# Batched A·Bᵀ in fp32: one start-up wait moved from TensorE to VectorE, and the closing waits moved from GpSimd to SyncE

## The chip, the cores and the metric

The kernel runs on one core of one Trainium2 chip. The time is the device time of one execution in microseconds. For the kernel before, six runs gave a median of 127.28 us, from 126.77 to 127.58 us. One further execution was profiled; it took 126.67 us.

## The reference

Sixteen independent products of 512 x 512 matrices are computed. Inputs and outputs are float32; the kernel multiplies in bf16 and accumulates in fp32.

```python
def reference(a, b):            # a: 16 x 512 x 512, b: 16 x 512 x 512
    return np.matmul(a, b.transpose(0, 2, 1)).astype(np.float32)
```

Both factors have their contraction index last. [...] 33.55 MB are read from HBM and 16.78 MB are written.

## The kernel before

The batch is worked off in 8 pairs of matrices. For each pair, one 2 MB transfer brings in the two matrices of `a` and another one the two of `b`; a transfer fills one of seven `ld` buffers, with 8 consecutive rows of the pair on each of the 128 partitions. The first transfer of `a` and the first of `b` are split into two halves of 1 MB, with a semaphore for each half (`s_ld` and `s_second`).

The kernel is written out by hand: every engine has its own list of instructions, and semaphores are the only link between the lists. All of it stands in one critical section, and a second, very short section follows it.

- SyncE (SP) issues all loads and all stores but the first, in the order of the string `ORDER` (L32). Nine load instructions stand at its head and wait for nothing. Each later load waits until its buffer has been read (L89, L91), and each store waits until its output block has been evicted (L104). SP works in order, so a store that waits holds the loads behind it.
- VectorE (DVE) casts each load to bf16, in two halves (L116 and L121), into `ha` for `a` and `hb` for `b`. The first half of a cast raises `s_half`; the second raises `s_ca` or `s_cb`. It also evicts the transposes of `b` (L126).
- TensorE (PE) runs a hardware loop of 8 rounds (L172). In each it does 64 transposes of 128 x 128 (L185), through the identity matrix `ident`, and 32 matmuls of 128 x 512 (L199). Its first instruction in each round waits for `s_ca`. [...]
- ScalarE (ACT) evicts the transposes of `a` (L137) and the products (L153), and issues the store of product 0 (L163).
- GpSimd (POOL) builds the identity at the start: a memset (L67) and a select (L69), each of which raises `s_set` by one.

PE's list begins with a wait for `s_set` to be 2 (L171), ahead of the loop.

The end has two parts. When an engine has finished its list in the first section, it takes part in an exchange of semaphores that all five engines run between the sections (L40 in the profile). In the second section (L212 to L214), GpSimd waits for the last seven stores, 9 to 15, each in one of the seven buffers `ob` with its own semaphore `s_st`. After that the program has a closing barrier of all engines (L240), which also clears the semaphores.

Of the kernel before, what the change touches and what calls it, by code (L numbers as in the profile page):

```python
# [10 lines left out]
def kernel(  # L11
# [6 lines left out]
    nc = tc.nc  # L18
    P = 128
    batch, M, K = a.shape  # L20
# [8 lines left out]
    NO = 7  # L29
# [7 lines left out]
    def sem(name):  # L37
        return tc.alloc_semaphore(name)

    with tc.tile_critical(no_gpsimd_drain=True):  # L40
# [10 lines left out]
        s_set = sem("s_set")  # L51
        s_ld = [sem(f"s_ld{i}") for i in range(NL)]
        s_second = [sem(f"s_second{i}") for i in range(2)]
        s_st = [sem(f"s_st{i}") for i in range(NO)]
# [24 lines left out]
        for what in ORDER:  # L79
            if what == "L":  # L80
                u, slot = n_ld // 2, n_ld % NL
                src = (a if n_ld % 2 == 0 else b)[2 * u:2 * u + 2].rearrange(
                    "e (p j) k -> (e p) j k", j=2 * J
                )
                if n_ld >= NL:

                    v = (n_ld - NL) // 2
                    if (n_ld - NL) % 2 == 0:
                        nc.sync.wait_ge(s_half, 2 * v + 2)  # L89
                    else:  # L90
                        nc.sync.wait_ge(s_tb, KO * v + 1)  # L91
                if n_ld < 2:
                    nc.sync.dma_start(
                        ld[slot][:, :J, :], src[:, :J, :]
                    ).then_inc(s_ld[slot], 16)
                    nc.sync.dma_start(
                        ld[slot][:, J:, :], src[:, J:, :]
                    ).then_inc(s_second[slot], 16)
                else:
                    nc.sync.dma_start(ld[slot][:], src).then_inc(s_ld[slot], 16)  # L100
                n_ld += 1
            else:
                slot = n_st % NO
                nc.sync.wait_ge(s_out, n_st + 1)  # L104
                nc.sync.dma_start(
                    out[n_st].rearrange("(p j) n -> p j n", j=J), ob[slot][:]
                ).then_inc(s_st[slot], 16)
                n_st += 1

        for u in range(pairs):
            for x, (h, s_c) in enumerate(((ha, s_ca), (hb, s_cb))):
                n = 2 * u + x
                nc.vector.wait_ge(s_ld[n % NL], 16 * (n // NL + 1))
                nc.vector.tensor_copy(  # L116
                    out=h[:, :J, :], in_=ld[n % NL][:, :J, :]
                ).then_inc(s_half, 1)
                if n < 2:
                    nc.vector.wait_ge(s_second[n], 16)  # L120
                nc.vector.tensor_copy(  # L121
                    out=h[:, J:, :], in_=ld[n % NL][:, J:, :]
                ).then_inc(s_c, 1)
            for ko in range(KO):
                nc.vector.wait_ge(s_tb, KO * u + ko + 1)
                nc.vector.tensor_copy(  # L126
                    out=tb[:, ko, :],
                    in_=tp[:, (2 * ko + 1) % 4].rearrange("k j p -> k (j p)"),
                ).then_inc(s_eb, 1)
# [38 lines left out]
        def take(s, n):  # L168
            nc.tensor.wait_ge(s, n).then_inc(s, -n)  # L169

        nc.tensor.wait_ge(s_set, 2)  # L171
        with nc.Fori(  # L172
            0, pairs, engines=[nc.tensor.engine], head_slot={nc.tensor.engine: 24}
        ):
# [33 lines left out]
                    t.then_inc(s_mm, 1)  # L208

    with tc.tile_critical(no_gpsimd_drain=True):  # L212
        for n in range(batch - NO, batch):
            nc.gpsimd.wait_ge(s_st[n % NO], 16 * (n // NO + 1))  # L214


# [28 lines left out]
```

## Time and profile before

| what | before |
|---|---|
| median of 6 runs | 127.28 us |
| lowest and highest run | 126.77 and 127.58 us |
| the profiled execution, whole | 126.67 us |
| its span, first to last instruction | 124.9 us |
| granted TensorE clock, mean | 0.982 |
| PE, DVE, ACT, POOL busy | 72%, 47%, 57%, 1% |
| data moved | 50.37 MB, 403 GB/s over the span |

The page of a profile lists the busy time of each engine, and cuts the span into 40 slices in which one digit is the busy share in tenths; the row named DMA is the mean over the core's 16 DMA engines. Its last parts name groups of instructions by source line, and DMA issues with the time from issue to landing. Further views of the trace used here are: the waits (who waited for whom), the instructions of one source line, the timeline, the DMA queues in a window of time, and the busy times in chosen windows. All times in them count from the span's first instruction. A name such as SPq or POOLq is the engine's sequencer: the instructions that only wait, branch or issue. A transfer of this kernel is split over the 16 DMA engines, and each adds one to the transfer's semaphore when its share has landed, so that the sixteenth part sets the landing.

### The profile page before, as it was taken

What the parts mean: (1) busy time and instruction counts of PE and PEld (TensorE: products, weight loads), DVE (VectorE), ACT (ScalarE), POOL (GpSimd) and SP (SyncE); (2) the same over time, 40 slices, a digit from 0 to 9 for tenths busy, and PEclk for the clock granted to TensorE, in tenths of its full rate; (3) what the DMA queues carried; (4) which work ended last, traced back from release to release, by engine and by line L of the source; (5) the groups of instructions that cost most, each with busy time, mean ns of one, the idle gap of its engine ahead of it and who ended that gap; (6) DMA issues with size and microseconds to landing.
All of it is one profiled execution on the core that took longest, in us unless ns stands there. A gap on an engine that the chain in (4) does not pass through costs nothing. (4 is left out here: it accounts for less than half of the span.)

```text
span 124.9 us, 1959 instructions
## 1 busy us (share of the span) xinstructions
PE 89.9 (72%) x768; PEld 56.7 (45%) x768; DVE 59.2 (47%) x64; ACT 70.7 (57%) x129; POOL 0.7 (1%) x6
## 2 busy tenths in 40 slices
PE   0003089799789969996999699969776999698000
PEld 0002089347644754484449345934374458343000
DVE  0034534971794287648905980690566566300000
ACT  4001225468937885696669567947755769567000
POOL 2000000000000000000000000000000000000000
PEclk9999999999999999999999999999999999999975
DMA  3999999999999999999999999999999999999980
GB/s 92 394 422 441 436 436 436 420 430 373 401 422 417 462 396 430 417 430 441 415 441 430 388 443 420 401 443 415 454 428 425 415 428 425 425 422 428 425 349 16
DMA packets 4899, 50.37 MB, mean 403 GB/s; under 512 B 544, under 2 KB 544, under 8 KB 544
## 3 DMA queue, kind: packets, MB, share of 16 engines
q1 hardware_dynamic: 4752, 49.29, 94.2%
q10 hardware_dynamic: 144, 1.05, 2.0%
q8 instruction: 1, 0.02, 0.0%
q14 instruction: 2, 0.02, 0.0%
HBM read 33.55 MB, written 16.78 MB: 403 GB/s over the span
## 5 line engine op out<-in xcount | busy, mean ns | idle before, releaser
L199 PE MATMUL ps<-tb,ta 128*128 128x512 bf16 x256 | 56.5, 379 | 8.3 <-PEq L169 8.3
L153 ACT COPY ob<-ps 128x512 f32<-128x512 f32 x64 | 37.5, 586 | 26.4 <-PE ps L199 26.4
L137 ACT COPY ta<-tp 128x512 bf16<-128x512 bf16 x64 | 32.6, 625 | 17.7 <-PE tp L185 17.7
L199 PEld LDWEIGHTS ps<-tb,ta 128*128 128x128 bf16 x256 | 24.5, 98 | 37.8 <-issue 9.4
L126 DVE COPY tb<-tp 128x1024 bf16<-128x1024 bf16 x32 | 22.1, 691 | 28.7 <-PE tp L185 28.7
L185 PE MATMUL tp<-ident,ha 128*128 128x128 bf16 x256 | 21.2, 230 | 11.1 <-PEq L169 11.1
L185 PE MATMUL tp<-ident,hb 128*128 128x128 bf16 x256 | 21.0, 228 | 5.8 <-PEq L169 5.8
L185 PEld LDWEIGHTS tp<-ident,ha 128*128 128x128 bf16 x256 | 17.1, 104 | 13.7 <-issue 11.1
L185 PEld LDWEIGHTS tp<-ident,hb 128*128 128x128 bf16 x256 | 16.9, 103 | 6.3 <-issue 6.3
L116 DVE CAST hb<-ld 128x2048 bf16<-128x2048 f32 x8 | 9.8, 1223 | 9.3 <-DMA ld<-in_b_dram 9.3
L116 DVE CAST ha<-ld 128x2048 bf16<-128x2048 f32 x8 | 9.8, 1219 | 7.0 <-DMA ld<-in_a_dram 7.0
L121 DVE CAST ha<-ld 128x2048 bf16<-128x2048 f32 x8 | 9.8, 1220 | 2.2 <-DMA ld<-in_a_dram 2.2
L121 DVE CAST hb<-ld 128x2048 bf16<-128x2048 f32 x8 | 9.8, 1220 | 1.3 <-DMA ld<-in_b_dram 1.3
L137 ACT ACT_TABLE_LOAD x1 | 1.3, 1283 | 0.9 <-SPq L40 0.9
L69 POOL TENSOR_SCALAR_AFFINE_SELECT ident<-ident 128x128 bf16<-128x128 bf16 x1 | 0.3, 292 | 0.2 <-POOL ident L67 0.2
L67 POOL MEMSET ident<- 128x128 bf16 x1 | 0.2, 204 | 0.5 <-SPq L40 0.5
L229 POOL MEMSET const-bfloat16-1.0<- 128x1 bf16 x1 | 0.1, 101 | 0.0
L229 POOL MEMSET const-uint8-127<- 128x1 uint8 x1 | 0.1, 101 | 0.0
L229 POOL MEMSET const-float32-0.0<- 128x1 f32 x1 | 0.1, 98 | 0.2 <-issue 0.2
L229 POOL MEMSET const-float32-1.0<- 128x1 f32 x1 | 0.1, 98 | 0.0
## 6 DMA issues: line engine op xcount, KB each, us to landing
out_dram<-ob SPq DMA_DIRECT2D x15, 1024.0 KB, 25.6
ld<-in_a_dram SPq DMA_DIRECT2D x7, 2048.0 KB, 30.2
ld<-in_b_dram SPq DMA_DIRECT2D x7, 2048.0 KB, 31.7
ld<-in_a_dram SPq DMA_DIRECT2D x2, 1024.0 KB, 6.8
ld<-in_b_dram SPq DMA_DIRECT2D x2, 1024.0 KB, 11.4
out_dram<-ob ACTq DMA_DIRECT2D x1, 1024.0 KB, 12.5
```

What stands on the lines that cost most here:

```text
L67: nc.gpsimd.memset(ident[:], 0.0).then_inc(s_set, 1)
L69: nc.gpsimd.affine_select(out=ident[:], in_=ident[:], compare_op=mybir.AluOpType.not_equal, fill=1.0, base=0, pattern=[[-1, P]], channel_m ...
L116: nc.vector.tensor_copy(out=h[:, :J, :], in_=ld[n % NL][:, :J, :]).then_inc(s_half, 1)
L121: nc.vector.tensor_copy(out=h[:, J:, :], in_=ld[n % NL][:, J:, :]).then_inc(s_c, 1)
L126: nc.vector.tensor_copy(out=tb[:, ko, :], in_=tp[:, (2 * ko + 1) % 4].rearrange("k j p -> k (j p)"),).then_inc(s_eb, 1)
L137: c = nc.scalar.copy(out=ta[:, ko, e * J * P:(e + 1) * J * P].rearrange("k (j p h) -> k j p h", j=J, h=2), in_=tp[:, (2 * ko) % 4, :, e * ...
L153: c = nc.scalar.copy(out=ob[i % NO][:, j, :].rearrange("m (p j) -> m p j", j=2 * J), in_=ps[:, j, :].rearrange("m (j p) -> m p j", j=2 * J),)
L185: t = nc.tensor.transpose(tp[:, (2 * ko + x) % 4, j, :], h[:, j, ko * P:(ko + 1) * P], ident[:],)
L199: t = nc.tensor.matmul(ps[:, j, :], ta[:, ko, (e * J + j) * P:(e * J + j + 1) * P], tb[:, ko, :].rearrange("k (j p) -> k j p", j=2 * J)[:, ...
L229: nc = _bacc.Bacc("TRN2", target_bir_lowering=False, num_devices=1)
```

## The change

There are two edits.

At the start, PE's wait for `s_set` is gone: PE goes into its loop directly. VectorE waits for `s_set` instead, ahead of its first cast. PE's first transpose still waits for `s_ca`, which VectorE raises after that cast, so the identity is ready by then.

At the end, GpSimd's seven waits in the second section are gone. SP waits for stores 9 to 14 at the end of its list in the first section, and for store 15 alone in the second section.

```diff
@@ in the first section, after SP's list
                 n_st += 1
-
-
-
+        for n in range(batch - NO, batch - 1):
+            nc.sync.wait_ge(s_st[n % NO], 16 * (n // NO + 1))
+
+
+
+        nc.vector.wait_ge(s_set, 2)
         for u in range(pairs):
@@ ahead of PE's loop
-        nc.tensor.wait_ge(s_set, 2)
         with nc.Fori(
             0, pairs, engines=[nc.tensor.engine], head_slot={nc.tensor.engine: 24}
         ):
@@ the second section
     with tc.tile_critical(no_gpsimd_drain=True):
-        for n in range(batch - NO, batch):
-            nc.gpsimd.wait_ge(s_st[n % NO], 16 * (n // NO + 1))
+        nc.sync.wait_ge(s_st[(batch - 1) % NO], 16 * ((batch - 1) // NO + 1))
```

[...] GpSimd's closing list before is six instructions with two waits each (seven stores and the engines' own semaphores of the exchange) and a branch with one; store 15 stands in the first of them. SP's new list in the first section is three instructions and a branch; in the second it is three more and a branch, with store 15 in the third.

## The prediction

> **What bounds the kernel now.** I read the page's slices first, then the queues, and then the two ends of the span. From the page (slices in tenths, then queue: packets, MB, share of the 16 engines):
>
> ```profile
> span 124.9 us, 1959 instructions
> ...
> DMA  3999999999999999999999999999999999999980
> ...
> q1 hardware_dynamic: 4752, 49.29, 94.2%
> q10 hardware_dynamic: 144, 1.05, 2.0%
> q8 instruction: 1, 0.02, 0.0%
> q14 instruction: 2, 0.02, 0.0%
> ```
>
> The DMA row is 9 from the second slice to the second last: the transfers are the bound, and no engine is. The busy times by window (us of the window, then each engine, granted clock, DMA share, GB/s) cut the span into the fill, the stream, the last store and the close:
>
> ```profile
> 0.00:1.96 1.96, 0.00 (x0) 0.00 (x0) 0.00 (x0) 1.06 (x1) 0.70 (x6) 1.00 0.02 4
> 1.96:115.69 113.73, 89.87 (x768) 56.74 (x768) 59.16 (x64) 69.61 (x129) 0.00 (x0) 1.00 1.01 422
> 115.69:123.06 7.37, 0.00 (x0) 0.00 (x0) 0.00 (x0) 0.00 (x0) 0.00 (x0) 0.82 0.76 322
> 123.06:124.90 1.84, 0.00 (x0) 0.00 (x0) 0.00 (x0) 0.00 (x0) 0.00 (x0) 0.50 0.00 0
> ```
>
> The first data packet starts at 1.96, the last store is issued at 115.69, and its last part lands at 123.06. At its issue some 7 us of stores are still queued, so compute is ahead of the DMA and a shift of compute under about 4 us (two stores of 2.43 us each lie before it) costs nothing. Behind the landing, 1.84 us pass in which nothing moves. The chain of work on the page stops at ACT's last eviction (115.08) and doesn't see this tail; SP's own waits do (total, times, longest):
>
> ```profile
> SPq L240 <- POOLq L212: 7.5, 1, 7.5
> ```
>
> So only three things can move the time: when the stream starts, how long the slowest of the 16 DMA engines needs, and the 1.84 us.
>
> **The end.** The rows of the closing line (duration min/median/max in ns, first to last start):
>
> ```profile
> L240 POOLq EVENT_SEMAPHORE  x9: 17/43/43, 123.2 to 124.8; - x9
> L240 SPq DRAIN  x3: 7/7/7, 123.9 to 124.3; - x3
> L240 POOLq COMPARE_BRANCH  x2: 33/33/33, 0.8 to 123.6; - x2
> ```
>
> GpSimd's first wait is released at 123.086, 24 ns after the landing. It stands first of six, and the other five, long satisfied, follow one by one at 87 ns: 123.18, .26, .35, .44, .52, and the branch at 123.61. Then come the semaphore for the section's end (123.76), two bookkeeping instructions (123.86, 123.95), a drain, and the gathering step of the barrier at 124.082. From landing to gathering: 1.02 us.
>
> After, the same path on SP, priced by SP's own rows: release 24 ns; from one wait to the next SP takes 74 ns (116.272 to 116.346); branch to next instruction 154 (0.788 to 0.942); semaphore to drain 77 (116.065 to 116.142); drain to the instruction that waits for it 130 (to 116.272); 69 to the next; one drain to the next 60 (123.941 to 124.001); then the hop to GpSimd, 8 + 40. Sum 24 + 74 + 154 + 77 + 130 + 69 + 60 + 48 = 0.64 us. **Gain 1.02 - 0.64 = 0.38 us.** The hop is the one part that before didn't have on its path (there GpSimd was its own last arrival): between 24 ns (a released wait) and 73 (the slowest reading, 124.009 to 124.082), so 0.35 to 0.40.
>
> SP's six waits in the first section are paid earlier. Store 14 lands at 120.63. Queued behind these waits on SP is only the section's end, and for that all other engines wait, which have no work left. They and the exchange between sections cost 0.2 + 0.42 (116.065 to 116.481), so SP stands at the wait for store 15 by about 121.4, 1.6 us ahead of 123.06. The cover is the transfer of store 15; without it 0.6 us would be paid in full. The gap between the landings of the stores is 2.43 us and steady, so it stays. GpSimd's seven waits vanish and nothing is queued behind them.
>
> **The start.** VectorE's new wait holds the first cast, and all of VectorE's list behind it. `s_set` is 2 at 1.68 us, and the first half load lands at 6.25: nothing to wait for. One more instruction of some 20 to 50 ns stands there; it is covered by the 2.24 us that VectorE waits before the second cast (9.74).
>
> What moves is PE's entry into the loop. Its rows (L172), and the DMA queues between 5.6 and 6.7 us:
>
> ```profile
> L172 PEldq COMPARE_BRANCH  x9: 76/208/298, 1.8 to 113.4; - x9
> ...
> L172 PEldq MOVE  x1: 29/29/29, 1.7 to 1.7; - x1
> ```
> ```profile
> q8 instruction: 1, 0.02, 5.3%
> ```
>
> PE waits with the MOVE until 1.706 and jumps at 1.793. At 5.686 one DMA engine reads 16 KB of instructions for 0.93 us, and its next packet takes 0.80 instead of 0.31. The jump is its likely cause: 3.89 us lie between, and ACT's store, [...] needs 3.81 (27.31 to 31.12). The price is seen in the landings: parts 1 to 15 of the second half load are in by 8.70, the sixteenth by 9.72. One part stays 1.0 us behind the next through the five transfers after it, too. After the change the MOVE comes right behind the branch of 0.82 to 1.00, the jump at about 1.1, 0.7 us earlier, so that the request can reach its engine before the first packets of 1.96.
>
> What that is worth at the end: in the last store the sixteenth part lands at 123.06 and the fifteenth at 122.76, 0.30 ahead of it. If the late engine is still the one of the fetch and the fetch no longer costs it anything, the next one sets the end: 0.30. Lower bound 0 (the 16 KB are still moved, or another engine is last); upper bound 0.93, the fetch itself, for executions where that engine is further behind. A loss is not excluded, since the fetch would delay that engine's first half load by up to 0.93 to 7.2; that is still before 9.7, so it costs nothing. I take 0.30, the row of the profile.
>
> [...] its first transpose starts at 11.09, released by the cast at 10.98. An earlier jump then gives PE itself nothing: [...] 0.30 by the rows, which say that the DMA engine is what suffers and not PE.
>
> **Sum.** 0.38 + 0.30 = 0.68. The profiled execution: 126.67 - 0.68 = 125.99, with 1.77 us around the span as before (span 124.9 to 124.2). It lies 0.61 below the median of the runs; nothing in the sum scales with that, so the median goes from 127.28 to **126.6**.
>
> **The rivals.** *The end alone*: the fetch comes among the first packets and costs its engine as much, or another engine is last. For it: the later spread of the 16 parts is 2.33 us, more than one fetch makes, so other delays take part. 127.28 - 0.38 = 126.9.
>
> *No gain*: the hand-over between engines eats what the five waits give. Against it: each step has a row; for it: closing barriers set by the latest of five engines have more than one way to be late. 127.3.
>
> *Slower, by SP's code*: the two 8 KB instruction packets (52.04 and 75.29) come when ACT stands at about its 46th instruction and DVE at its 45th, 3.8 us earlier each: [...] SP's list had 48 in all, and its 46th fell into the closing barrier; with nine or so more it falls at about 121.3, just ahead of the wait for store 15. If SP had to wait there for code at the 3.9 us that PE's packet took to start, it would go on at 125.2, 2.1 after the landing: 127.28 + 2.1 - 0.38 = 129.0. It decides from a stall of 1.8 us on. [...]
>
> **How the numbers follow.** Chances: sum as forecast 0.45, end alone 0.28, no gain 0.13, slower 0.14 (with whatever else delays the stream). A change of 0.5% (0.64 us) is about what a measurement of this kernel can tell from none. The forecast lies just beyond it, and its start term may be larger than taken: three quarters of it count as faster, 0.34. Of the end alone a third does, since six runs scatter over 0.8 us: 0.10. Faster 0.44; same 0.11 + 0.18 + 0.13 = 0.42; slower 0.14. The range: below, 0.38 + 0.93 gives 126.0; above, no gain with 0.3 of scatter gives 127.6. The forecast's own range is 126.0 to 126.9.
>
> **What would show it.** End: from the last landing to GpSimd's gathering step 0.64 us instead of 1.02, and the last window 1.46 instead of 1.84 us; SP at its last wait by 121.5 or so. Start: PE's jump at 1.1; the instruction packet well before 5.7; the second half load complete at 8.7 and the second cast at 8.7, 1.0 earlier; the last store's sixteenth part within 0.1 of the fifteenth. The start term is wrong if the packet merely moves and its engine still lags by 1.0; the end term is wrong if SP reaches its last wait after the landing, or a gap appears in SP's list at about 121.3.

## The result and the profile after

The changed kernel takes 126.72 us in the median of 36 runs (126.21 to 127.37), the kernel before 127.33 us in 73 runs (126.55 to 128.01). The ratio is 0.9957, with a 95% interval from 0.9945 to 0.9969: 0.55 us less, between 0.39 and 0.70. That is inside the forecast's range, 0.1 us above its point. The interval leaves out 1, although the change is just short of the 0.5% that the forecast called measurable.

The page's slices and queues have not changed their shape, so the stream of transfers is still the bound:

```profile
span 125.1 us, 1960 instructions
...
DMA  4999999999999999999999999999999999999970
...
q8 instruction: 1, 0.02, 0.0%
q14 instruction: 2, 0.02, 0.0%
```

The span of this one execution is longer than that of before, 125.1 to 124.9 us, while the median is shorter. The windows of the changed kernel show how both can be true (fill, stream, last store, close; us of the window, then the engines, clock, DMA share, GB/s):

```profile
1.96:115.95 113.99, 88.65 (x768) 55.54 (x768) 59.54 (x64) 69.53 (x129) 0.00 (x0) 1.00 1.01 422
115.95:123.80 7.85, 0.00 (x0) 0.00 (x0) 0.00 (x0) 0.00 (x0) 0.00 (x0) 0.61 0.68 286
123.80:125.11 1.31, 0.00 (x0) 0.00 (x0) 0.00 (x0) 0.00 (x0) 0.00 (x0) 0.50 0.00 0
```

The last part of the last store landed at 123.80, 0.74 us later than in the profile of before. Over the eleven traces of this study that landing lies between 123.00 and 123.87, in no order by kernel. It is the scatter of the last of the store's sixteen parts, 0.87 us, and it is larger than the whole effect. The close behind the landing is the part that the kernel decides, and it hardly scatters: to the nanosecond of the trace it is 1.826 us before and 1.317 after. The start's edit alone, with the old end, has 1.826 again, and the five other traces with the new end all have 1.317.

The rows of the closing line say why (ns min/median/max, first to last start):

```profile
L240 SPq EVENT_SEMAPHORE  x5: 17/28/1692, 122.0 to 125.1; - x5
L240 POOLq EVENT_SEMAPHORE  x4: 17/17/17, 124.3 to 125.0; - x4
...
L240 SPq COMPARE_BRANCH  x2: 33/33/33, 0.8 to 123.9; - x2
```

GpSimd's nine semaphore instructions have become four, and the first of them starts at 124.3: that is the gathering step of the barrier, at which GpSimd waits for the other engines. From there to the end of the span all eleven traces need 0.80 or 0.81 us. SP's long one, 1.69 us, holds the wait for store 15. From landing (123.798) to gathering step (124.310) the trace has 0.51 us, where before had 1.02. SP's waits show where its time goes now (total, times, longest):

```profile
SPq L110 <- DMA out_dram<-ob: 4.8, 2, 2.4
SPq L240 <- DMA out_dram<-ob: 1.7, 1, 1.7
```

The waits of the first section take 4.8 us, all of it before the last landing, and SP stands at its last wait at 122.13, 1.7 us ahead of it.

At the start, PE's jump into its loop moved from 1.793 to 1.141, and the packet of 16 KB of instructions with it, from 5.686 to 3.690. In the view of the DMA queues from 3.6 to 4.7 us it is

```profile
q8 instruction: 1, 0.02, 5.3%
```

and the timeline of the start shows the price (start, duration, engine and line, idle before):

```profile
7.19 1.23 DVE L119 CAST ha<-ld 128x2048 bf16<-128x2048 f32 x1 [7.19 <-DMA ld<-in_a_dram]
9.62 1.23 DVE L124 CAST ha<-ld 128x2048 bf16<-128x2048 f32 x1 [1.20 <-DMA ld<-in_a_dram]
10.96 0.77 PEld L187 LDWEIGHTS tp<-ident,ha 128*128 128x128 bf16 x8 [10.96 <-issue]
```

The first cast starts at 7.19 where it was 6.28 before, since the sixteenth part of the first half load lands at 7.09, 1.0 us behind the fifteenth. The second cast starts at 9.62 (before: 9.74). So the packet came sooner, and one of the sixteen parts is still 1.0 us behind the next, as before. It is taken here for the part of the DMA engine that read the packet: where the packet fell behind these loads, at 118.22 us in the last experiment, all sixteen parts land within 0.67 us.

### The profile page after: what moved, and what is told of

It is laid out like the page before. It is cut to its first block, busy times and chain, and to the rows that moved or that the text cites. A ratio compares the mean times of both kernels' runs of the same rounds, so it can differ in the third digit from the quotient of the medians.

```text
span 125.1 us, 1960 instructions
## 1 busy us (share of the span) xinstructions
PE 88.6 (71%) x768; PEld 55.5 (44%) x768; DVE 59.5 (48%) x64; ACT 70.6 (56%) x129; POOL 0.7 (1%) x6
## 5 line engine op out<-in xcount | busy, mean ns | idle before, releaser
L187 PE MATMUL tp<-ident,ha 128*128 128x128 bf16 x256 | 20.5, 225 | 11.0 <-PEq L172 11.0
L187 PE MATMUL tp<-ident,hb 128*128 128x128 bf16 x256 | 20.4, 225 | 7.1 <-PEq L172 7.1
L187 PEld LDWEIGHTS tp<-ident,ha 128*128 128x128 bf16 x256 | 16.5, 101 | 13.6 <-issue 11.0
L187 PEld LDWEIGHTS tp<-ident,hb 128*128 128x128 bf16 x256 | 16.3, 101 | 7.7 <-issue 7.7
```

Source lines behind the costliest of these rows:

```text
L187: t = nc.tensor.transpose(tp[:, (2 * ko + x) % 4, j, :], h[:, j, ko * P:(ko + 1) * P], ident[:],)
```

## The experiments

The theory from the traces: **all of the gain is the end's**, and it is the number of instructions between the last landing and the barrier that counts. The rivals are the forecast's own split, in which the start gives a part, and the idea that SP is simply a better place to wait than GpSimd.

### One edit at a time

The end's edit alone:

```diff
+        for n in range(batch - NO, batch - 1):
+            nc.sync.wait_ge(s_st[n % NO], 16 * (n // NO + 1))
...
-        for n in range(batch - NO, batch):
-            nc.gpsimd.wait_ge(s_st[n % NO], 16 * (n // NO + 1))
+        nc.sync.wait_ge(s_st[(batch - 1) % NO], 16 * ((batch - 1) // NO + 1))
```

> The kernel before with the end's edit alone: SP waits for stores 9 to 14 in the first section and for store 15 in the second; PE keeps its wait for the identity. If all of the gain is the end's (0.51 us from landing to the gathering step in the trace of after, 1.02 in the one of before): ratio 0.996, 0.51 us less. If the forecast's split holds (end 0.38, start the rest of 0.55): ratio 0.997. In the trace, both: 0.51 us from the last landing to the gathering step, and the 16 KB instruction packet back at about 5.7 us.

Measured: 126.38 against 127.22 us, 0.9936 (0.9910 to 0.9962). The trace has 0.514 us from landing to gathering step, and the instruction packet at 6.09.

The start's edit alone:

```diff
+        nc.vector.wait_ge(s_set, 2)
         for u in range(pairs):
...
-        nc.tensor.wait_ge(s_set, 2)
         with nc.Fori(
```

> The kernel before with the start's edit alone: VectorE waits for the identity, PE doesn't. If all of the gain is the end's: ratio 1.000. If the start gives a part (0.17 to 0.30 us): 0.9976 to 0.9987. In the trace: the instruction packet at about 3.7 us, its DMA engine's part 1.0 us behind the next in the first half load already, and 1.02 us from landing to gathering.

Measured: 127.28 against 127.22 us, 1.0001 (0.9983 to 1.0020). The trace has the packet at 4.12, the sixteenth part of the first half load at 7.53 with the fifteenth at 6.22, and 1.020 us from landing to gathering step. GpSimd's nine semaphore instructions are back:

```profile
L240 POOLq EVENT_SEMAPHORE  x9: 17/43/43, 123.7 to 125.3; - x9
```

The packet moved as in the changed kernel, and no gain is seen; one of 0.30 us (0.9976) lies outside the interval, one of 0.17 us just inside. Here the last part lags by 1.3 us.

The first value of the end alone was lower than that of the whole change, which left open that the early packet costs something. Both were therefore run side by side on one chip.

> The end's edit alone once more, now beside the changed kernel on the same chip. Its first measurement was 0.9936, the changed kernel's 0.9957, with intervals that overlap. If the start edit costs nothing, both come out alike, 0.995 to 0.996; if the early instruction packet costs something, this one stays 0.2 to 0.3 us below the changed kernel.

> The changed kernel itself, beside the end's edit alone on the same chip. If the start edit is worth nothing: 0.995 to 0.996, within 0.1 us of the end's edit alone. If it costs 0.2 to 0.3 us: 0.9965 to 0.998 where the other has 0.994 to 0.995.

Measured, against 126.97 us: the end alone 126.63, 0.9966 (0.9949 to 0.9983); the changed kernel 126.42, 0.9947 (0.9932 to 0.9961). Now the order is the other way round, with intervals that overlap. Weighting the two values of each kernel by their intervals gives 0.9957 for the end alone and 0.9953 for both edits. The two can't be told apart over both measurements: about 0.2 us either way for the start's edit is what these runs leave open.

### Engine or number of waits

GpSimd keeps the waiting, but split in the same way:

```diff
+        for n in range(batch - NO, batch - 1):
+            nc.gpsimd.wait_ge(s_st[n % NO], 16 * (n // NO + 1))
...
-        for n in range(batch - NO, batch):
-            nc.gpsimd.wait_ge(s_st[n % NO], 16 * (n // NO + 1))
+        nc.gpsimd.wait_ge(s_st[(batch - 1) % NO], 16 * ((batch - 1) // NO + 1))
```

> The kernel before with GpSimd still as the waiting engine, but split as in the change: stores 9 to 14 at the end of GpSimd's list in the first section, store 15 alone in the second. If what counts is how many waits follow the landing (87 ns each on GpSimd), five of them are gone: 1.02 - 0.44 = 0.58 us from landing to gathering, ratio 0.9966. If it is that SP is the faster engine or hears the barrier sooner, hardly anything: 0.999 to 1.000.

Measured: 126.86 against 127.22 us, 0.9969 (0.9949 to 0.9989). The closing line of this kernel reads

```profile
L241 POOLq EVENT_SEMAPHORE  x7: 17/17/1860, 121.9 to 125.1; - x7
...
L241 POOLq COMPARE_BRANCH  x2: 33/33/33, 0.8 to 123.9; - x2
```

with store 15 landing at 123.871, the branch at 123.946 and the gathering step at 124.416: 0.545 us. GpSimd does nearly as well as SP once no satisfied wait follows the landing.

SP in GpSimd's place, with all seven waits in the second section:

```diff
         for n in range(batch - NO, batch):
-            nc.gpsimd.wait_ge(s_st[n % NO], 16 * (n // NO + 1))
+            nc.sync.wait_ge(s_st[n % NO], 16 * (n // NO + 1))
```

> The kernel before with SP in GpSimd's place and all seven waits in the second section. If the number of waits counts, five waits of about 65 ns still follow the landing: 0.51 + 0.33 = 0.84 us to the gathering step, ratio 0.9986. If it is the engine that counts, nearly all of the gain: 0.51 to 0.58 us and 0.996.

Measured: 127.11 against 127.22 us, 0.9985 (0.9967 to 1.0003). The closing line of this kernel:

```profile
L240 SPq EVENT_SEMAPHORE  x7: 17/28/28, 123.1 to 124.6; - x7
L240 POOLq EVENT_SEMAPHORE  x4: 17/17/17, 123.8 to 124.5; - x4
...
L240 SPq COMPARE_BRANCH  x2: 33/33/33, 0.8 to 123.4; - x2
```

Six wait instructions follow the landing at 123.002, 62 ns apart on average (123.018 to 123.324, and the branch at 123.392), and the gathering step comes 0.847 us after the landing. With all seven waits behind the landing, SP in GpSimd's place saves 0.173 us: 25 ns for each wait instruction, 87 to 62, and 0.01 us in the steps after them. Taking the waits away from there saves another 0.333 us on SP (the end's edit alone) and 0.475 on GpSimd. So the number of waits counts for more than the engine.

SP with all seven in the first section:

```diff
+        for n in range(batch - NO, batch):
+            nc.sync.wait_ge(s_st[n % NO], 16 * (n // NO + 1))
...
-        for n in range(batch - NO, batch):
-            nc.gpsimd.wait_ge(s_st[n % NO], 16 * (n // NO + 1))
+        nc.sync.wait_ge(s_set, 2)
```

> The kernel before with SP waiting for all seven stores, 15 among them, at the end of the first section; the second section holds a wait of SP for the identity's semaphore, satisfied since the start. The exchange between the sections and the second section's own list then follow the landing: from SP's rows in the trace of after, 0.15 (branch) + 0.30 (exchange, 121.554 to 121.854) + 0.08 + 0.20 (three waits) + 0.51 less the 0.03 of the first release and wait = about 1.2 us to the gathering step. If the split is what earns the gain: ratio 1.000 to 1.002, no gain at all. If it is enough that SP waits instead of GpSimd: 0.996 to 0.998.

Measured: 127.31 against 126.97 us, 1.0027 (1.0012 to 1.0043), slower than before by 0.15 to 0.55 us. The windows around its last landing:

```profile
115.90:123.26 7.36, 0.00 (x0) 0.00 (x0) 0.00 (x0) 0.00 (x0) 0.00 (x0) 0.78 0.72 303
123.26:125.39 2.13, 0.00 (x0) 0.00 (x0) 0.00 (x0) 0.00 (x0) 0.00 (x0) 0.50 0.00 0
```

The close takes 2.13 us, since the exchange between the sections and the second section's list now follow the landing: 1.328 us to the gathering step. What the change does right is to leave one store out of the first section, so that the exchange runs under it.

Together, the path from landing to gathering step and the time:

| kernel | landing to gathering step, us | less than before, us | as a share of the time | ratio measured |
|---|---|---|---|---|
| before | 1.020 | | | 1 |
| start's edit alone | 1.020 | 0 | 1.0000 | 1.0001 |
| SP, all in the first section | 1.328 | -0.308 | 1.0024 | 1.0027 |
| SP, all in the second section | 0.847 | 0.173 | 0.9986 | 0.9985 |
| GpSimd, split | 0.545 | 0.475 | 0.9963 | 0.9969 |
| end's edit alone | 0.514 | 0.506 | 0.9960 | 0.9936, 0.9966 |
| the change | 0.512 | 0.508 | 0.9960 | 0.9957, 0.9947 |

The third column is the difference from 1.020, and the fourth divides it by 127.3 us. For every row the share from the trace lies within the interval of each measured ratio. One number from the trace is enough for all of these times.

### Where the instruction packet falls

A wait for the first half cast, ahead of PE's loop in the changed kernel:

```diff
+        nc.tensor.wait_ge(s_half, 1)
         with nc.Fori(
```

> The changed kernel with one wait more ahead of PE's loop: for the first half cast (s_half), which ends at about 7.5 us. If PE's jump is what calls for the 16 KB of instructions, the packet moves from 3.7 to about 10 to 11.5 us, and the second half load is complete by 8.7 instead of 9.6, with the second cast at about 8.7. If something else calls for it, it stays at 3.7. The time: if where the packet falls doesn't matter, 0.996 as after; if an early packet costs something at the end, less than after by up to 0.3 us (0.9935).

Measured: 126.59 against 126.97 us, 0.9977 (0.9961 to 0.9994). PE's rows for the loop's line, and the DMA queues from 10.9 to 12.1 us, are

```profile
L175 PEldq COMPARE_BRANCH  x9: 76/208/298, 7.6 to 114.9; - x9
```
```profile
q8 instruction: 1, 0.02, 5.2%
```

The jump is at 7.555 and the packet at 11.016. The packet has followed the jump each time: from 1.793 to 1.141 it went from 5.686 to 3.690, and with the jump at 7.555 it comes at 11.016. The timeline of the start:

```profile
6.20 1.23 DVE L119 CAST ha<-ld 128x2048 bf16<-128x2048 f32 x1 [6.20 <-DMA ld<-in_a_dram]
8.62 1.23 DVE L124 CAST ha<-ld 128x2048 bf16<-128x2048 f32 x1 [1.19 <-DMA ld<-in_a_dram]
9.96 0.77 PEld L188 LDWEIGHTS tp<-ident,ha 128*128 128x128 bf16 x8 [9.96 <-issue]
```

Without the packet in the first loads, the second cast comes at 8.62 and PE's first transposes at 9.96, 1.0 us earlier than after the change. The time does not fall. If anything it is longer than that of the changed kernel on the same chip (0.9932 to 0.9961 there, 0.9961 to 0.9994 here), which no branch of the expectation had; why, was not tried. PE works on its loop at 9.96, 1.06 us before the packet has begun, so in this trace the packet does not hold the code with which the loop starts.

The changed kernel without the loop's `head_slot`, which was meant to let PE run straight into the body:

```diff
         with nc.Fori(
-            0, pairs, engines=[nc.tensor.engine], head_slot={nc.tensor.engine: 24}
+            0, pairs, engines=[nc.tensor.engine]
         ):
```

> The changed kernel without the fixed slot for the loop's head, so that the body follows PE's entry code directly instead of being jumped to. Where the 16 KB packet then falls isn't known. [...] If there is none and its 1.0 us on one DMA engine counts at the end: 0.9925 to 0.994. If it doesn't count, or the packet only comes later: 0.995 to 0.997. [...]

Measured: 127.00 against 127.33 us, 0.9974 (0.9950 to 0.9998). The packet comes at 118.22, 3.4 us after PE's last branch in its loop (114.863); the queues from 118.1 to 119.2 us show it:

```profile
q8 instruction: 1, 0.02, 5.3%
```

The second cast comes earlier still:

```profile
8.44 1.23 DVE L124 CAST ha<-ld 128x2048 bf16<-128x2048 f32 x1 [1.18 <-DMA ld<-in_a_dram]
```

All loads up to 28 us land with their sixteen parts within 0.67 us, where the changed kernel has 1.8. Yet the last store again ends with a spread of 2.93 us, at 123.66. Other delays, most of them between 43 and 86 us, have put other parts behind by then: the spread is 0.53 us at 43, 1.38 at 49 and 2.47 at 89. What these delays are was not tried.

This trace also bears on where the packet's own engine stands at the end. Set against the parts of store 14 in order, fifteen parts of store 15 land about 2.44 us later, and one lands 3.69 us later (118.76 to 122.45), 1.25 us more than the others. It is taken for the part of the engine that read the packet at 118.22, and it is still 1.2 us ahead of the sixteenth. On that reading the engine that read the packet was not the one that set the end in this execution. In the other traces the parts can't be followed through the mixed loads and stores from 29 to 49 us, so whether it is the last one there stays open. No run leaves the read out altogether.

## Why the prediction was right, and where it was not

**What bounds the kernel** held. PE's first transposes came 1.0 us earlier in the run with the late entry, and the time did not fall. At the other end, SP issues the last store between 115.69 and 117.35 us in the eleven traces, and a late issue does not make a late landing: the trace with the latest issue lands at 123.53, and the changed kernel's, with 115.95, at 123.80.

**The end** held in its mechanism and was sized too small: 0.38 forecast, 0.51 measured. The term that was off is SP's path from landing to gathering step, 0.64 in the sum and 0.51 in the trace. Step by step, forecast and trace: release and step to the branch 98 and 60 ns; branch 154 and 155; to the drain 77 and 85; from the drain on 130 and 73; next 69 and 44; drain to drain 60 and 64; hop 48 and 31. The largest miss is the drain. Its price came from the row at 116.142, where it took 56 ns, 0.45 us after a store was issued; here it took 7, after a wait of 1.7 us. The same split runs through the drain at the first section's end: 56 or 57 ns in the four kernels in which SP goes there from the store, 7 in the seven in which it waits for stores first. The next is the step from the last wait to the branch, forecast at 74 and measured at 38. The hop was 31 ns, within its bounds of 24 and 73.

**The cover** held: SP stood at its last wait at 122.13, not 121.4 as forecast, because in this execution store 14 landed 0.7 us later, at 121.32; the last landing was 0.7 later too. The exchange is hidden, and the run with all waits in the first section shows what it costs uncovered: 1.328 - 0.512 = 0.82 us, more than the 0.6 that the prediction named, since the second section's list comes out from under the store as well.

**The start** was wrong. That the packet comes with the jump is shown by three positions of the jump (1.14, 1.79 and 7.56 us, with the packet 2.55, 3.89 and 3.46 us behind), and the kernel without `head_slot` has its one packet at 118.22, 3.4 us behind PE's last branch. That an earlier jump would spare the DMA engine the packet's cost is not: the step that failed is "the fetch no longer costs it anything". The forecast took it that the packet would be read ahead of the first packets of 1.96 us. It came at 3.69, 2.0 us sooner than before but in the middle of the first half load, and one part lagged by 1.0 as before. The forecast had named this case as a loss that costs nothing, with the first half load put off to as much as 7.2 us; 7.09 was measured. The next step, that the engine of the fetch is the one that sets the end, is not shown for any run and, on the reading above, is wrong for the kernel without `head_slot`. Where the packet came at 11 or at 118 us the end did not come earlier either.

A reason for all of these zeros is the author's estimate from the rows and was not tested. From 1.96 us to the last store's issue the DMA share is 1.01 on average, so the engines hardly idle there. If the one that reads the 16 KB does not idle at all, its work is the same wherever in that stretch the 0.93 us of the read fall.

For PE itself an earlier jump gave nothing, as forecast. Its first weight load starts 0.11 us behind the end of the second cast in these four traces, whose packets lie far apart:

| kernel | packet, us | second cast starts, us | PE's first weight load, us |
|---|---|---|---|
| before | 5.69 | 9.74 | 11.09 |
| the change | 3.69 | 9.62 | 10.96 |
| late entry | 11.02 | 8.62 | 9.96 |
| without `head_slot` | 118.22 | 8.44 | 9.78 |

The cast takes 1.23 us in each. So at the start PE follows the cast here, wherever the packet falls.

So of the rivals the end alone is what happened, with an end larger than it assumed: 127.33 - 0.51 = 126.8 for the measured 126.72. The point of 126.6 came close by luck, since two errors of opposite sign met: 0.13 too little for the end and 0.30 too much for the start.

**No gain** is excluded by the interval. **Slower, by SP's code** did not occur: around its 46th instruction SP goes from step to step at 121.854, 121.933 and 122.002 without a gap, and the page still has two instruction packets in q14 and no third. ACT ran on evenly at the same place in its list: in the kernel before, its 46th, 47th and 48th instructions are evictions at 47.66, 48.52 and 49.39, 0.86 us apart.

## What to carry to other kernels

In a kernel whose end is a landing, count the instructions between that landing and the final barrier: each wait instruction that is already satisfied still cost 62 ns on SP and 87 on GpSimd here. Let all other waits, and the exchange between sections, run while the last transfer is under way, and leave only that transfer for the end. When an effect of half a microsecond lies under a landing that scatters by 0.87, read it from the stretch that the edit touches, not from the span of one profile.

## What the runs showed that was not expected

One read of 16 KB of instructions took 0.93 us on one DMA engine, before and after the change. Where it fell among the first loads, it left one part of every later load up to 29 us behind the next by 0.9 to 1.3 us. Still, moving the read to 3.7, 11 or 118 us gained nothing at the end. A jump 0.65 us earlier moved the read by 2.0 us, and when the jump was at 7.6 the read followed 3.5 us later. So the wait that held PE's jump back was worth a microsecond to the first loads here: the late entry's second half load was complete at 8.59 us, the changed kernel's at 9.59. In this kernel the first loads do not set the time; one in which they do was not tried.
